# An encoder block on one core: all tiles at the right end of the on-chip memory placed 224 bytes lower

## The chip, the core and the metric

The kernel runs on one core of one Trainium2 chip. The metric is the device time of one execution in microseconds (us), as the median of several runs. The on-chip memory has 128 partitions; an address in this text is a byte offset within a partition, and the same offset holds in all 128. "32 past" means that an address divided by 64 leaves 32, "even" that it leaves 0.

## The reference

One layer on 512 tokens of width 1024, batch 1, all in float32:

```python
xn = rms_norm(h, g_mix);  proj = xn @ w_in                  # (512, 2048)
b_gate, c_gate, v_conv, u_pool = the four 512-wide parts of proj
h = h + concat([b_gate * conv3(c_gate * v_conv), pool_mixer(u_pool)]) @ w_o
xb = rms_norm(h, g_ffn);  q = xb @ w_q                      # 8 heads, 2 halves of 128
s = q . sub_keys                     # 128 keys a half; top 16 of each half, then top 16 of the 256 sums
h = h + sum over the chosen e of softmax(score)_e * gelu(u_e . xb) * v_e     # 16384 experts
h = h + sigmoid(rms_norm(h, g_ple) @ w_ple_gate) * (p @ w_ple_proj)
out = rms_norm(h, g_final)
```

## The kernel before

Everything is one program, `block_kernel`, for one core. Large products are made from float32 numbers split in two parts: a high part H that ScalarE (ACT) writes in the rounded format fp32r, and a low part L = raw - H that VectorE (DVE) writes. A product is then three matmuls (`mm3`: H·H at L123, H·L at L125, L·H at L127), or, in `mm3_pair`, two such products with their matmuls interleaved. In a profile row such as `acc<-xH,wH` the first name after the arrow is the tile that TensorE (PE) streams through, the second is the tile that it holds as weights; each matmul has a weight load of its own (PEld).

The stages, in order of time in the profiled execution:

1. **Start and mixer, 0 to about 160 us.** `norm_rows` and `xT_chunk` make the normalised, transposed input in the tiles xH and xL. Eight pieces of w_in (256 columns each: wraw, split into wH and wL) are weights against the streamed xH, xL, 512 columns a matmul (`projT`). The mixers write mixH and mixL. For the output projection the roles turn round: mixH, mixL are weights and the pieces of w_o are streamed, 256 columns a matmul. Beside it `ple` multiplies pT by wp and stores the result from the tiles pleo.
2. **Queries and keys, to about 279 us.** Eight pieces of w_q, again as weights wH, wL against streamed xH, xL with 512 columns; then 16 matmuls a head against the tile keys, and the top-16 searches on DVE.
3. **First pass over the experts, to about 652 us.** 76 blocks of 128 experts: uraw is loaded, split into uH, uL (weights), and xH, xL are streamed, 384 columns a matmul (`score`). In between run the rest of the top-k on DVE, one-hot matmuls (tiles oh, gg) whose result is collected in stage and stored by ACT's queue, and row gathers by POOL into the six buffers gr for one token block of 128.
4. **Second pass, to about 1397 us.** For the other blocks `score` as before; for all 128 blocks `mix`: wH, wL of the pool wq as weights, the halves of vH, vL streamed, 512 columns a matmul, into the results o.
5. **Tail, to the end.** For each of four token blocks 8 transposes (`tail_T`), giving tH and tL as weights, against the split w_gate, which lies in the former places of xH, xL (first half) and uraw, uH, uL (second half): 512 columns a matmul for seven half blocks, and 256 for two quarters of the last block (`tail_gate`, list QS).

**Where tiles lie.** Pools take memory from the left end (low addresses) or, with `side="right"`, from the right end downwards, each pool on the last one that is open. The right end that the allocator gives is byte 229,344, which is 32 past. Most sizes are multiples of 64, so most right tiles begin 32 past; in the mixer's pool wk the tile zb takes 2080 bytes, which is not such a multiple, and the tiles below it (pT to zb) begin even. The name wH stands for two sets of tiles: the pieces of w_in, w_o and w_q (pool w, right), and those of the second pass (pool wq, left).

The order on each engine is set by the scheduler of the framework for stages 1 to 3 (from a model of times) and is program order from the second pass on (`manual_schedule`). The right side's first pool in the code is

```python
    hpool = sh.enter_context(tc.tile_pool(name="h", bufs=1, side="right"))
```

Of the kernel before, what the change touches and what calls it, by code (L numbers as in the profile page):

```python
# [7 lines left out]
F32 = mybir.dt.float32  # L8
# [8 lines left out]
P = 128  # L17
# [43 lines left out]
def block_kernel(ctx: ExitStack, tc: tile.TileContext, x, pT_in, g_cols, w_in, conv_w, pool_w,  # L61
# [4 lines left out]
    consts = ctx.enter_context(tc.tile_pool(name="consts", bufs=1))  # L66
    dram = ctx.enter_context(tc.tile_pool(name="dram", bufs=1, space=bass.MemoryType.DRAM))
    small = ctx.enter_context(tc.tile_pool(name="small", bufs=2))
    sbx = ExitStack()
    xpool = sbx.enter_context(tc.tile_pool(name="xt", bufs=1))  # L70
    sh = ExitStack()
# [926 lines left out]
```

## Time and profile before

| | us |
|---|---|
| median of 3 runs | 1455.18 (1454.88 to 1456.47) |
| the profiled execution | 1454.46 |
| its span (first to last recorded instruction) | 1452.7 |
| PE busy, matmuls | 1430.8 (98%) |
| DVE busy | 1137.7 (78%) |
| ACT busy | 614.5 (42%) |
| POOL busy | 390.7 (27%) |
| mean granted TensorE clock | 0.994 |

Times in rows count from the start of the span. Matmuls overlap in the records, so a matmul's duration (390 ns for 512 columns, say) is not what it costs: that is read from the distance of the starts of consecutive matmuls. A row of the timeline merges equal neighbours (x2).

### The profile page before, as it was taken

The numbers are of one execution on the slowest core, as the hardware profiler recorded it, in microseconds if no ns is written. First come the engines' busy times: TensorE is split into PE (matmuls) and PEld (weight loads), VectorE is DVE, ScalarE is ACT, GpSimd is POOL, SyncE is SP. The second block draws the span as 40 slices with busy tenths as digits, with TensorE's granted clock in tenths as the row PEclk, the third lists the DMA queues.
The fourth block names the chain that finished last, engine by engine and source line by source line (L and its number), as shares of the span: only waits on it lengthen the run. The fifth ranks groups of instructions, "written<-read, shape, count | busy, mean of one in ns | idle before, by whom it ended". The sixth has DMA issues, their size and how long they took to land.

```text
span 1452.7 us, 20601 instructions
## 1 busy us (share of the span) xinstructions
PE 1430.8 (98%) x7785; PEld 1271.6 (88%) x7785; DVE 1137.7 (78%) x2078; ACT 614.5 (42%) x864; POOL 390.7 (27%) x260
## 2 busy tenths in 40 slices
PE   8999999999998999999999999999999999999997
PEld 5789888999998999998999999999998888788886
DVE  5644579899998987879988778888877777776765
ACT  5321533344564665664333333333333334433354
POOL 0000000002132132125766555454443123342000
PEclk9999999999998999999999999999999999999999
DMA  8223730047688899899998999998997899998721
GB/s 302 87 90 104 242 116 30 30 164 279 227 285 268 274 316 326 262 317 347 380 349 323 375 329 339 347 339 324 346 336 273 317 334 333 335 342 324 249 70 73
DMA packets 152083, 381.38 MB, mean 263 GB/s; under 512 B 10928, under 2 KB 72112, under 8 KB 151728
## 3 DMA queue, kind: packets, MB, share of 16 engines
q1 hardware_dynamic: 72400, 211.75, 41.3%
q0 software_dynamic: 36864, 134.23, 25.3%
q10 hardware_dynamic: 42720, 34.08, 7.2%
q8 instruction: 61, 1.00, 0.3%
q14 instruction: 38, 0.31, 0.1%
HBM read 339.92 MB, written 40.11 MB: 262 GB/s over the span
## 4 chain that ended last, share of the span: by engine, by line
PE 71%; DVE 12%; DMA 7%; issue 6%; ACT 2%; POOL 1%; ACTq 1%; SPq 0%; DVEq 0%; POOLq 0%
PE o L127 11%; PE o L123 11%; PE o L125 11%; PE acc L125 6%; PE acc L123 6%; PE acc L127 6%; PE u L127 5%; PE u L123 5%; PE u L125 5%; DMA uraw<-in_u_blk 3%; DVE uL L586 2%; DMA tH<-in_w_gate 2%; POOL gr L536 1%; PE acc L191 1%; PE tp L516 1%
## 5 line engine op out<-in xcount | busy, mean ns | idle before, releaser
L536 POOL DMA_INDIRECT gr<-in_u_rows,eidx x128 | 201.1, 1571 | 652.5 <-DVE tsm L390 334.6
L536 POOL DMA_INDIRECT gr<-in_v_rows,eidx x128 | 189.4, 1480 | 285.2 <-DVE xrow L560 274.5
L125 PE MATMUL o<-vL,wH 128*128 128x512 f32 x768 | 237.2, 390 | 0.7 <-DVE vL L604 0.7
L123 PE MATMUL o<-vH,wH 128*128 128x512 f32 x768 | 237.7, 390 | 0.3 <-ACT wH L685 0.3
L127 PE MATMUL o<-vH,wL 128*128 128x512 f32 x768 | 237.3, 390 | 0.1
L598 ACT ACTIVATE vH<-vraw 128x1024 fp32r<-128x1024 f32 x128 | 135.4, 1058 | 218.3 <-PE o L127 160.8
L123 PE MATMUL acc<-xH,uH 128*128 128x384 f32 x608 | 206.6, 340 | 3.4 <-ACT uH L580 3.4
L604 DVE TENSOR_TENSOR vL<-vraw,vH 128x1024 fp32r<-128x1024 f32 x128 | 156.2, 1221 | 65.2 <-ACT vH L598 64.9
L125 PE MATMUL acc<-xL,uH 128*128 128x384 f32 x608 | 206.8, 340 | 0.0
L127 PE MATMUL acc<-xH,uL 128*128 128x384 f32 x608 | 204.7, 339 | 0.2 <-DVE uL L586 0.2
L580 ACT ACTIVATE uH<-uraw 128x1024 fp32r<-128x1024 f32 x128 | 135.3, 1058 | 100.6 <-DMA uraw<-in_u_blk 64.0
L586 DVE TENSOR_TENSOR uL<-uraw,uH 128x1024 fp32r<-128x1024 f32 x128 | 155.7, 1217 | 24.8 <-ACT uH L580 24.8
L125 PEld LDWEIGHTS o<-vL,wH 128*128 128x128 f32 x768 | 144.0, 188 | 32.3 <-DVE vL L604 1.5
L127 PEld LDWEIGHTS o<-vH,wL 128*128 128x128 f32 x768 | 143.9, 188 | 31.2 <-DVE wL L690 1.0
L560 DVE SCALAR_TENSOR_TENSOR xrow<-gr,gate,xrow 128x1024 f32<-128x1024 f32 x128 | 164.1, 1282 | 5.1 <-DMA xrow<-h_d 4.6
L123 PEld LDWEIGHTS o<-vH,wH 128*128 128x128 f32 x768 | 143.3, 188 | 27.2 <-ACT wH L685 0.7
L556 DVE SCALAR_TENSOR_TENSOR gr<-gr,xrow 128x1024 f32<-128x1024 f32 x128 | 154.3, 1218 | 4.2 <-DMA gr<-in_u_rows,eidx 4.1
L127 PE MATMUL u<-xH,uL 128*128 128x384 f32 x416 | 139.6, 336 | 0.0
L123 PE MATMUL u<-xH,uH 128*128 128x384 f32 x416 | 139.5, 335 | 0.0
L125 PE MATMUL u<-xL,uH 128*128 128x384 f32 x416 | 139.3, 335 | 0.0
L123 PEld LDWEIGHTS acc<-xH,uH 128*128 128x128 f32 x608 | 115.4, 190 | 4.1 <-ACT uH L580 4.1
L127 PEld LDWEIGHTS acc<-xH,uL 128*128 128x128 f32 x608 | 115.1, 189 | 0.8 <-DVE uL L586 0.8
(214 smaller groups left out, 2336.8 us busy)
## 6 DMA issues: line engine op xcount, KB each, us to landing
uraw<-in_u_blk SPq DMA_DIRECT2D x128, 512.0 KB, 5.2
vraw<-in_v_rows SPq DMA_DIRECT2D x128, 512.0 KB, 6.0
G_d<-stage ACTq DMA_DIRECT2D x12, 1664.0 KB, 12.8
gq<-G_d SPq DMA_DIRECT2D x26, 768.0 KB, 7.0
A_d<-a ACTq DMA_DIRECT2D x17, 768.0 KB, 6.0
aq<-A_d SPq DMA_DIRECT2D x17, 768.0 KB, 9.5
wraw<-in_w_in SPq DMA_DIRECT2D x8, 1024.0 KB, 5.8
wraw<-in_w_q SPq DMA_DIRECT2D x8, 1024.0 KB, 5.8
```

The lines of the kernel that those rows point to most:

```text
L123: nc.tensor.matmul(ps, lh, rh, start=start, stop=False)
L125: nc.tensor.matmul(ps, lh, rl, start=False, stop=False)
L127: nc.tensor.matmul(ps, ll, rh, start=False, stop=stop)
L191: nc.tensor.matmul(ps, pT[:, c, t * P:(t + 1) * P], wp[hf][:, c], start=c == 0, stop=c == 1)
L516: nc.tensor.matmul(ps[:, o:o + P], qb[b][:, t * P:(t + 1) * P], keys[:, 2 * hd + b], start=True, stop=True)
L536: nc.gpsimd.indirect_dma_start(out=g, out_offset=None, in_=table, in_offset=bass.IndirectOffsetOnAxis(ap=eidx[:, k:k + 1], axis=0))
L556: ins = nc.vector.scalar_tensor_tensor(g, g, 1.0, xrow, op0=OP.mult, op1=OP.mult, accum_out=act[:, k:k + 1])
L560: ins = nc.vector.scalar_tensor_tensor(accg, g, gate3[:, k - P:k - P + 1], accg, op0=OP.mult, op1=OP.add)
L580: nc.scalar.activation(ublk[i][1], ublk[i][0], AF.Copy)
L586: nc.vector.tensor_tensor(ublk[i][2], raw, uh.bitcast(F32), op=OP.subtract)
L598: nc.scalar.activation(vblk[n][1], vblk[n][0], AF.Copy)
L604: nc.vector.tensor_tensor(vblk[n][2], raw, vh.bitcast(F32), op=OP.subtract)
```

## The change

A pool is opened on the right side ahead of all others, and one tile of 56 float32 numbers (224 bytes a partition) is taken from it and never used. All later right tiles lie 224 bytes lower. Left tiles stay.

```diff
     small = ctx.enter_context(tc.tile_pool(name="small", bufs=2))
+    right = ctx.enter_context(tc.tile_pool(name="right", bufs=1, side="right"))
+    right.tile([P, 56], F32, name="rpad")
     sbx = ExitStack()
```

The byte addresses in the two built programs (first buffer of each; the others follow at multiples of the tile's size):

| tile | use | before | after | |
|---|---|---|---|---|
| wH, wL (pool w) | weights in w_in, w_q; streamed in w_o | 180192, 196576 | 179968, 196352 | 32 past -> even |
| mixH, mixL | weights in w_o | 114656, 131040 | 114432, 130816 | 32 past -> even |
| xs; keys; h | transposes; keys; residual | 147424; 118752; 212960 | 147200; 118528; 212736 | 32 past -> even |
| oh, gg; stage | one-hot matmuls; their store | 112608, 120800; 128992 | 112384, 120576; 128768 | 32 past -> even |
| gr; gres; a4 | gathers; results | 204768; 167904; 155616 | 204544; 167680; 155392 | 32 past -> even |
| tH, tL; gq | weights in the tail; transposes | 176096, 184288; 192480 | 175872, 184064; 192256 | 32 past -> even |
| pT, wp, pleo, pw, inv, pu, pm | mixer | 63232, 67328, 75520, 83712, 85760, 93952, 100288 | each 224 less | even -> 32 past |
| xH, xL; uraw, uH, uL | left | 16128, 32512; 48896, 57088, 69376 | the same | even |
| vraw, vH, vL; wH, wL (pool wq) | left | 81664, 93952, 106240; 130816, 136960 | the same | even |
| ident | streamed in transposes, left | 13984 | the same | 32 past |

The tiles that are "32 past" before lie at 224 above a multiple of 256, and after at a multiple of 256, as the left tiles named do. The instructions of every engine stand in the same order in both programs, with line numbers two higher in the changed one. One wait moves: the left tiles of the top-k and of uL share places with the mixer's right tiles of an earlier stage, and the 224 bytes shift that overlap. On DVE, where stage 1 gives way to stage 2, before:

```order
L586 TENSOR_TENSOR uL<-uraw,uH 128x1024 [waits DMAHW4_49,Activation_49]
L139 SCALAR_TENSOR_TENSOR xL<-g,gcol,xH 128x512 [waits Activation_49]
L139 SCALAR_TENSOR_TENSOR xL<-tp,gcol,xH 128x512 [waits Activation_49]
L335 TENSOR_TENSOR xrow<-xs 128x1024 [waits DMAHW6_49,DVE_49]
L586 TENSOR_TENSOR uL<-uraw,uH 128x1024 [waits DMAHW3_49,DMAHW5_49,DMAHW2_49,Activation_49]
L586 TENSOR_TENSOR uL<-uraw,uH 128x1024 [waits DMAHW7_49,Activation_49]
L97 TENSOR_TENSOR wL<-wraw,wH 128x2048 [waits DMAHW1_49,PE_49,Activation_49]
L348 MAX tv<-s 128x8 [waits DMAHW0_49,Activation_49]
```

and now the same place:

```order
L588 TENSOR_TENSOR uL<-uraw,uH 128x1024 [waits DMAHW4_49,Activation_49]
L141 SCALAR_TENSOR_TENSOR xL<-g,gcol,xH 128x512 [waits Activation_49]
L141 SCALAR_TENSOR_TENSOR xL<-tp,gcol,xH 128x512 [waits Activation_49]
L337 TENSOR_TENSOR xrow<-xs 128x1024 [waits DMAHW6_49,DVE_49]
L588 TENSOR_TENSOR uL<-uraw,uH 128x1024 [waits DMAHW3_49,DMAHW2_49,DMAHW5_49,DMAHW0_49,Activation_49]
L588 TENSOR_TENSOR uL<-uraw,uH 128x1024 [waits DMAHW7_49,Activation_49]
L99 TENSOR_TENSOR wL<-wraw,wH 128x2048 [waits DMAHW1_49,PE_49,Activation_49]
L350 MAX tv<-s 128x8 [waits Activation_49]
```

The wait for one DMA semaphore (DMAHW0) stands three rows earlier, at the second of the three uL shown instead of the first MAX; it belongs to a store of pleo to memory, whose place the new uL now touches.

## The prediction, made before the changed kernel ran

> **What bounds the kernel now.** I read the page's busy times and chain first, then who waits for whom on PE, then the starts of single matmuls in the timeline, stage by stage.
>
> ```profile
> span 1452.7 us, 20601 instructions
> PE 1430.8 (98%) x7785; PEld 1271.6 (88%) x7785; DVE 1137.7 (78%) x2078; ACT 614.5 (42%) x864; POOL 390.7 (27%) x260
> PE 71%; DVE 12%; DMA 7%; issue 6%; ACT 2%; POOL 1%; ACTq 1%; SPq 0%; DVEq 0%; POOLq 0%
> ...
> PE acc L191 <- DMA wp<-in_w_proj: 7.0, 1, 7.0
> PE acc L123 <- ACT uH L580: 3.4, 3, 2.6
> PE g L470 <- ACT stage L477: 1.4, 4, 0.4
> ```
>
> PE is busy for 1430.8 of 1452.7 us. Of what it waits for, 7.0 us is the first load and 3.4 us three late uH; no other entry is above 1.4. So DVE, ACT and transfers matter only where they make PE wait, and the time is the sum of the matmuls' starting distances. The change adds and moves no instruction, so it can only act through a price that depends on an address. The question is which operation has one.
>
> **Engines and transfers: no sign of a price.** DVE and ACT rows exist with all tiles even, and with tiles 32 past:
>
> ```profile
> L586 DVE TENSOR_TENSOR uL<-uraw,uH 128x1024 fp32r<-128x1024 f32 x128 | 155.7, 1217 | 24.8 <-ACT uH L580 24.8
> L556 DVE SCALAR_TENSOR_TENSOR gr<-gr,xrow 128x1024 f32<-128x1024 f32 x128 | 154.3, 1218 | 4.2 <-DMA gr<-in_u_rows,eidx 4.1
> L580 ACT ACTIVATE uH<-uraw 128x1024 fp32r<-128x1024 f32 x128 | 135.3, 1058 | 100.6 <-DMA uraw<-in_u_blk 64.0
> L113 ACT ACTIVATE xs<-h 128x1024 f32<-128x1024 f32 x8 | 8.4, 1054 | 10.5 <-DMA h<-in_x 6.0 <-DVE h L316 3.2 <-DVE nt L106 1.4
> ```
>
> uL (all even) takes 1217 ns, the pass over gr (read and written 32 past) 1218; uH (even) 1058, xs from h (both 32 past) 1054. So 0 for DVE and ACT, with at most 4 ns an instruction either way, hidden under PE. For transfers, the queues:
>
> ```profile
> q1 hardware_dynamic: 72400, 211.75, 41.3%
> q0 software_dynamic: 36864, 134.23, 25.3%
> q10 hardware_dynamic: 42720, 34.08, 7.2%
> ```
>
> A share is of 16 engines over 1452.7 us. POOL's gathers (q0, all into gr, 32 past) cost 0.253 x 16 x 1452.7 / 134.23 = 43.8 us of engine time per MB; q1, mostly loads into even tiles, 45.3. So 0 for the gathers. ACT's queue (q10, stores from right tiles, mostly in pieces of 512 bytes) costs 49.1, 8% above q1: if all of that were the address, the 3.4 us of waits for uH are the most that it could give back directly. I take 0.
>
> **Matmuls: here the rows differ.** First and last rows of undisturbed stretches, two each: w_in, second pass, tail with 512 columns, tail with 256, w_o, first pass, and the second pass's very end.
>
> ```profile
> 86.07 0.63 PE L123 MATMUL acc<-xH,wH 128*128 128x512 f32 x2
> 97.74 0.63 PE L125 MATMUL acc<-xL,wH 128*128 128x512 f32 x2
> ...
> 1129.99 0.62 PE L123 MATMUL o<-vH,wH 128*128 128x512 f32 x2
> 1141.32 0.62 PE L125 MATMUL o<-vL,wH 128*128 128x512 f32 x2
> ...
> 1423.78 0.40 PE L125 MATMUL o<-xL,tH 128*128 128x512 f32 x1
> 1436.85 0.40 PE L123 MATMUL o<-xH,tH 128*128 128x512 f32 x1
> ...
> 1440.82 0.28 PE L125 MATMUL o<-uL,tH 128*128 128x256 f32 x1
> 1444.43 0.28 PE L127 MATMUL u<-uH,tL 128*128 128x256 f32 x1
> ...
> 139.75 0.28 PE L125 MATMUL acc<-wL,mixH 128*128 128x256 f32 x1
> 140.95 0.28 PE L127 MATMUL acc<-wH,mixL 128*128 128x256 f32 x1
> ...
> 299.75 0.33 PE L125 MATMUL acc<-xL,uH 128*128 128x384 f32 x1
> 301.83 0.33 PE L125 MATMUL acc<-xL,uH 128*128 128x384 f32 x1
> ...
> 1394.89 0.62 PE L125 MATMUL o<-vL,wH 128*128 128x512 f32 x2
> 1396.71 0.62 PE L127 MATMUL o<-vH,wL 128*128 128x512 f32 x2
> ```
>
> - w_in: 25 pairs between the rows, 11.67 us / 50 = 233.4 ns a matmul. Weights 32 past, streamed tile even.
> - Second pass: also 25 pairs, 11.33 / 50 = 226.6. Both even.
> - Tail, 512 columns: 56 steps, 13.07 / 56 = 233.4. Weights 32 past, streamed even.
> - Tail, 256 columns: 31 steps, 3.61 / 31 = 116.5. Weights 32 past, streamed even.
> - w_o, 256 columns: 10 steps, 120.0. Both 32 past.
> - First pass, 384 columns: 12 steps, 2.08 / 12 = 173.3. Both even.
>
> Two lines come out. Where both tiles stand alike, 512, 384 and 256 columns cost 226.6, 173.3 and 120.0: 53.3 for each 128 columns, and w_o, with both 32 past, lies on it. Where only the weights are 32 past, 512 and 256 cost 233.4 and 116.5, a straight rate that is dearer by 6.8 at 512 and cheaper by 3.5 at 256. Surroundings do not explain it: the last mix matmuls run at 4 pairs in 1.82 us, 227.5 each, in the same quiet end where the tail has 233.4. Output banks do not (second pass and tail both write o), nor the streamed tile's name (x in the w_in pieces, u and uraw too in the tail). What the dear stretches share is the weights' address.
>
> **The change, term by term.** Afterwards wH, wL, tH, tL are even, the streamed tiles stay even, so I price them on the first line.
> 1. Weights of w_in and w_q: 768 matmuls of 512 columns (8 + 8 pieces x 2 halves x 8 x 3; the group rows of L123, L125 and L127 have 256 each) x 6.8 ns = -5.2 us.
> 2. Tail, 512 columns: 7 half blocks x 24 = 168, x 6.8 = -1.1 us.
> 3. Tail, 256 columns: 48, x 3.5 = +0.2 us.
> 4. w_o, keys, one-hot: both tiles move together; the first lies on the line already. 0.
> 5. The 64 + 32 transposes (xs, gq even afterwards, ident stays 32 past) come to stand unlike, and the mixer's pT, wp, pw, pm go from even to 32 past together. No row prices either; by the 3% (6.8 of 226.6) between the lines, either way, on some 30 us of PE time (17.3 of it L191): 0, with ±0.9 as bounds.
> 6. The moved DVE wait:
>
> ```profile
> L193 SPq DMA_DIRECT2D ple_d<-pleo x4: 319/320/320, 163.8 to 168.7; - x4
> DMA to landing us min/median/max: 5.8/5.9/7.9
> ...
> 181.00 1.22 DVE L586 TENSOR_TENSOR uL<-uraw,uH 128x1024 fp32r<-128x1024 f32 x1
> ```
>
> The last of these stores is issued at 168.7 and lands at most 7.9 us later, at 176.6; the uL that now waits for it starts at 181.00. I take 0. Were the store late, this uL, the next one, wL and the top-k would stand behind it on DVE, and PE would wait for that wL.
>
> Does the first 5.2 us reach the end? DVE could eat it, since it is nearly full when the first pass starts:
>
> ```profile
> 268.00:281.00 13.00, 13.00 (x74) 11.95 (x73) 10.31 (x71) 3.53 (x6) 0.00 (x0) 1.00 0.00 1
> 281.00:294.00 13.00, 13.00 (x77) 13.00 (x76) 13.00 (x82) 5.79 (x8) 0.00 (x0) 1.00 0.31 93
> 279.10 0.88 DVE L348 MAX8 tv<-s 128x8 f32<-128x128 f32 x4 [2.69 <-ACT s L518]
> ```
>
> (columns: PE, PEld, DVE, ACT, POOL busy). Until 281 DVE has idle time (10.31 of 13.00) and at 279.10 it has waited 2.69 us for the last head's scores, which come from PE through ACT. So DVE's full stretch starts when PE lets it, and slides with PE; the loads of uraw follow the buffers that DVE frees. I take the whole.
>
> Sum: -5.2 - 1.1 + 0.2 = -6.1 us, on the profiled execution's 1454.46: 1448.4. The median of the runs is 0.7 above that execution, so 1455.2 - 6.1 = 1449.1.
>
> **What may disturb it** is one place in the first pass:
>
> ```profile
> 445.00:450.00 5.00, 2.76 (x27) 2.28 (x25) 4.66 (x9) 1.82 (x2) 2.75 (x2) 0.99 0.95 392
> 450.00:455.00 5.00, 4.31 (x23) 3.87 (x24) 3.69 (x5) 4.55 (x10) 0.07 (x1) 0.50 0.97 337
> 455.00:460.00 5.00, 5.00 (x26) 5.00 (x25) 4.59 (x6) 0.51 (x2) 1.28 (x1) 0.82 1.08 322
> 460.00:465.00 5.00, 4.41 (x35) 3.85 (x34) 1.18 (x2) 2.11 (x4) 0.40 (x1) 1.00 0.55 183
> 465.00:470.00 5.00, 4.11 (x25) 3.82 (x25) 5.00 (x8) 3.95 (x8) 0.66 (x1) 0.70 0.56 194
> ```
>
> PE idles 2.24 + 0.69 + 0.59 + 0.89 = 4.4 us here (late uH and uL behind slow loads; DMA share 0.95 to 1.08), and the granted clock falls to 0.50, 0.82 and 0.70 for stretches of 5 us: another 2.5 + 0.9 + 1.5 = 4.9 lost. The place as a whole costs 9.3 us, and hangs on when loads meet stores. A shift by 5 us may soften or double it.
>
> **The rivals.**
> - *No effect.* The weights' address is only what the dear stretches happen to share; their place in the upper half of the memory, or something of the split tiles, makes the 6.8. Then nothing moves: 1455.2. For it: no row shows the same two tiles at two offsets. Against: seven stretches on two lines. [...]
> - *The stores get cheaper too.* If a start at a multiple of 256 shortens the stage stores, uraw lands earlier and the place at 445 to 470 vanishes: 1449.1 - 9.3 = 1439.8. For it: 8% on q10. Against: that 8% goes as well with the small pieces. [...]
> - *Slower.* The first pass starts 5 us earlier, loads and stores meet otherwise in it, and the place at 445 to 470 comes twice: 1449.1 + 9.3 = 1458.4. It decides as soon as what it adds exceeds the 6.1 saved. For it: uL there is late by little; against: everything that feeds it slides together.
>
> **How the numbers follow.** The forecast has 0.62, no effect 0.22, cheaper stores 0.08, slower 0.08. The likeliest case alone runs from 1446 to 1452 (terms 5 and part of the 9.3). The range takes in no effect up to the highest run shown, and leaves out the two last cases: 1444 to 1456.4. A difference under 0.2% (2.9 us) can't be told from none. Faster: 0.62 + 0.08, less 0.02 where the disturbed place eats most of it: 0.68. Slower: 0.08 and a little of no effect: 0.09. The rest, 0.23, is the same.
>
> **What would show it.** Right: starting distances of 226 to 227 ns in w_in, w_q and the tail, 120 in the tail's 256 columns, w_o unchanged, and the first score some 5 us earlier. Wrong in the step "weights' address": 233 stays. Wrong in the step "it reaches the end": 227 appears, but the gain is gone by 660 us, with more idle PE or half clock between 350 and 650. A new distance in w_o, keys or one-hot would show that standing alike is not what counts.

## The result, and the profile after

The changed kernel takes 1447.79 us (median of 7 runs, 1446.25 to 1451.91) against 1455.27 for the kernel before (7 runs beside it): ratio 0.9944, interval 0.993 to 0.9957, which by the ratio is 8.1 us less (6.3 to 10.2); the two medians are 7.5 us apart. The forecast was 1449.1. The profiled execution took 1447.79.

From the page of the changed kernel (span, busy times, queues) and the view of who waits for whom on PE:

```profile
span 1446.0 us, 20600 instructions
PE 1422.0 (98%) x7785; PEld 1267.6 (88%) x7785; DVE 1137.4 (79%) x2078; ACT 612.7 (42%) x864; POOL 381.1 (26%) x260
q1 hardware_dynamic: 72400, 211.75, 41.0%
q0 software_dynamic: 36864, 134.23, 25.4%
q10 hardware_dynamic: 42720, 34.08, 7.0%
...
PE acc L193 <- DMA wp<-in_w_proj: 6.9, 1, 6.9
PE g L472 <- ACT stage L479: 2.9, 8, 0.7
PE acc L125 <- ACT uH L582: 2.9, 4, 1.7
```

PE is 8.8 us less busy. DVE and ACT stand where they were, and the three queues within 0.3 points. The starts of matmuls in the timeline (start, duration), in the places shown of before: w_in, second pass, tail with 512 columns, tail with 256, w_o.

```profile
86.06 0.62 PE L127 MATMUL acc<-xL,wH 128*128 128x512 f32 x2
97.40 0.39 PE L129 MATMUL acc<-xH,wL 128*128 128x512 f32 x1
...
1123.18 0.61 PE L125 MATMUL o<-vH,wH 128*128 128x512 f32 x2
1134.06 0.61 PE L125 MATMUL o<-vH,wH 128*128 128x512 f32 x2
...
1417.12 0.39 PE L125 MATMUL o<-xH,tH 128*128 128x512 f32 x1
1430.71 0.39 PE L125 MATMUL o<-xH,tH 128*128 128x512 f32 x1
...
1433.75 0.28 PE L129 MATMUL o<-uH,tL 128*128 128x256 f32 x1
1437.11 0.28 PE L125 MATMUL u<-uH,tH 128*128 128x256 f32 x1
...
136.88 0.28 PE L129 MATMUL acc<-wH,mixL 128*128 128x256 f32 x1
138.32 0.28 PE L129 MATMUL acc<-wH,mixL 128*128 128x256 f32 x1
```

w_in goes from 233.4 to 11.34 / 50 = 226.8 ns, the tail from 233.4 to 13.59 / 60 = 226.5 and at 256 columns from 116.5 to 3.36 / 28 = 120.0. The second pass stays (10.88 / 48 = 226.7), and w_o too (1.44 / 12 = 120.0). These are the numbers that the prediction gave for tiles that stand alike.

Where the span's 6.7 us come from, by the first matmul of each stage (first w_in, first score, first row of the second pass, first of the tail, last of all). Before:

```profile
18.84 0.47 PE L123 MATMUL acc<-xH,wH 128*128 128x512 f32 x1
273.31 0.33 PE L123 MATMUL acc<-xH,uH 128*128 128x384 f32 x1
660.21 0.63 PE L123 MATMUL o<-vH,wH 128*128 128x512 f32 x2
1397.95 0.48 PE L123 MATMUL o<-xH,tH 128*128 128x512 f32 x1
1444.43 0.28 PE L127 MATMUL u<-uH,tL 128*128 128x256 f32 x1
```

and after:

```profile
18.55 0.48 PE L125 MATMUL acc<-xH,wH 128*128 128x512 f32 x1
268.40 0.33 PE L125 MATMUL acc<-xH,uH 128*128 128x384 f32 x1
653.40 0.63 PE L125 MATMUL o<-vH,wH 128*128 128x512 f32 x2
1392.08 0.48 PE L125 MATMUL o<-xH,tH 128*128 128x512 f32 x1
1437.71 0.28 PE L129 MATMUL u<-uH,tL 128*128 128x256 f32 x1
```

So -0.29 us ahead of w_in, -4.62 in w_in, w_o and w_q (254.47 to 249.85), -1.90 in the first pass, +0.94 in the second, -0.85 in the tail. The experiments ask two things: what rule of addresses lies behind the 6.6 ns, and whether the 1.90 and 0.94 belong to the change.

### The profile page after: what moved, and what is told of

The parts are those of the page before. It is cut to its first block, busy times and chain, and to the rows that moved or that the text cites. A ratio compares the mean times of both kernels' runs of the same rounds, so it can differ in the third digit from the quotient of the medians.

```text
span 1446.0 us, 20600 instructions
## 1 busy us (share of the span) xinstructions
PE 1422.0 (98%) x7785; PEld 1267.6 (88%) x7785; DVE 1137.4 (79%) x2078; ACT 612.7 (42%) x864; POOL 381.1 (26%) x260
## 4 chain that ended last, share of the span: by engine, by line
PE 48%; DVE 4%; DMA 4%; issue 2%; ACT 1%; SPq 0%; DVEq 0%; ACTq 0%
PE o L125 10%; PE o L129 10%; PE o L127 10%; PE u L129 5%; PE u L125 5%; PE u L127 5%; DMA tH<-in_w_gate 4%; DVE vL L606 2%; DVE xrow L562 1%; PE acc L127 1%; PE acc L129 1%; DVE aq L682 1%; PE acc L125 1%; DVE wL L692 0%; ACT xH L98 0%
## 5 line engine op out<-in xcount | busy, mean ns | idle before, releaser
L538 POOL DMA_INDIRECT gr<-in_u_rows,eidx x128 | 197.1, 1540 | 649.7 <-DVE tsm L392 329.7
L538 POOL DMA_INDIRECT gr<-in_v_rows,eidx x128 | 183.9, 1437 | 292.4 <-DVE xrow L562 281.7
L588 DVE TENSOR_TENSOR uL<-uraw,uH 128x1024 fp32r<-128x1024 f32 x128 | 155.8, 1218 | 29.8 <-ACT uH L582 29.4
L558 DVE SCALAR_TENSOR_TENSOR gr<-gr,xrow 128x1024 f32<-128x1024 f32 x128 | 154.3, 1218 | 2.5 <-DMA gr<-in_u_rows,eidx 2.5
```

Of the source, the lines that this page charges most:

```text
L538: nc.gpsimd.indirect_dma_start(out=g, out_offset=None, in_=table, in_offset=bass.IndirectOffsetOnAxis(ap=eidx[:, k:k + 1], axis=0))
L558: ins = nc.vector.scalar_tensor_tensor(g, g, 1.0, xrow, op0=OP.mult, op1=OP.mult, accum_out=act[:, k:k + 1])
L588: nc.vector.tensor_tensor(ublk[i][2], raw, uh.bitcast(F32), op=OP.subtract)
```

## The experiments

The stages of their profiled executions, in us, each number the difference of two starts read as above. The kernels are described one by one below; after_again is the changed kernel once more, and mix32_timed is the kernel of mix32_again once more. Two tiles are called like when their starts leave the same remainder against 64 bytes, and unlike when they don't. A ratio is a kernel's time over that of the kernel before in runs beside it, with its 95% interval in brackets.

| kernel | first w_in to first score | first pass | second pass | tail |
|---|---|---|---|---|
| before | 254.47 | 386.90 | 737.74 | 46.48 |
| after | 249.85 | 385.00 | 738.68 | 45.63 |
| after_again | 249.84 | 386.65 | 738.28 | 45.63 |
| early | 249.97 | 385.49 | 739.26 | 46.48 |
| late | 254.36 | 385.92 | 735.76 | 45.63 |
| left32 | 251.30 | 387.03 | 739.27 | 45.87 |
| w2_unlike | 254.48 | 384.13 | 748.92 | 46.48 |
| mix32 | 249.95 | 383.34 | 737.99 | 45.63 |
| mix32_again | 248.63 | 384.06 | 735.31 | 45.63 |
| mix32_timed | 248.64 | 386.05 | 738.02 | 45.63 |
| mix64 | 248.92 | 387.14 | 738.53 | 45.63 |

**1. Matmuls alone, first grid.**

```
for w, s in pairs: 24 x matmul(bank[r % 2], W[w][:, slice r % 4], S[s], start=True, stop=True)
```

> A kernel of matmuls alone, 24 in a row of each kind, over weights (letter after w) and streamed tiles (letter after s) that start 0, 4, 8, 16, 32, 48, 64 or 128 bytes (a to h) past a multiple of 64; its output leaves out the whole block and is mostly x. Theory 'alike' (what counts is whether both tiles stand the same way against 64 bytes): the pairs aa, dd, ee, ff at 512 columns take 226.6 ns each and every unlike pair 233.4; at 256 columns alike 120.0, unlike 116.5; at 384 alike 173.3 and unlike 175.0 (on the straight rate of 0.456 ns a column); ag, ga, gg, ah, ha as aa. Theory 'weights alone' (only the weights' start counts): all pairs with a in front 226.6, and all with e in front 233.4, ee too. Theory '256 bytes' (a larger grid counts): ag, ga, ah or ha come out at 233.4. Theory 'no address' (the name or the stage made the 6.8 ns): all pairs the same.

Each kind begins where the row of its first matmul starts, so the next kind's start less its own, over 24, is its price (in a row: streamed tile, then weights):

```profile
63.62 0.39 PE L100 MATMUL pu<-sd,wd 128*128 128x512 f32 x1
69.20 0.40 PE L100 MATMUL pu<-se,wd 128*128 128x512 f32 x1
...
85.85 0.39 PE L100 MATMUL pu<-sd,we 128*128 128x512 f32 x1
91.45 0.39 PE L100 MATMUL pu<-se,we 128*128 128x512 f32 x1
96.91 0.39 PE L100 MATMUL pu<-sf,we 128*128 128x512 f32 x1
```

With the same weights 32 past, an unlike stream costs 233.3 (sd) and the like one 227.5 (se): "weights alone" and "no address" fall. But sd,wd, both 16 past, costs 232.5 where "alike" wanted 226.6, and starts 64 bytes apart do not cost the same as 0: 229.0 with the stream ahead, 233.3 with the weights ahead. So against 64 is not the rule. With tiles in the two-byte format f16 the starts 0 and 32 past cost the same within 0.5: 216.3 for the first pair, 215.8 for the other three.

**2. Second grid: the distance in steps of 32 bytes.** Only the starts differ from the first.

> Matmuls alone once more (the output leaves out the whole block), now over the distance of the two starts: letters a to p stand for 0 to 480 bytes in steps of 32 past a multiple of 512, x, y and z for 0 in tiles elsewhere. First the streamed tile is moved, then the weights, then both together; the first series comes again at the end in reverse order. Theory '64 bytes' (alike against 64 is enough): a, c, e, g, ... all at 226.6 ns for 512 columns, the others at 233.4. Theory '256 bytes' (the distance against 256 counts, as 229 ns with a distance of 64 bytes and 232 with 128 in the first grid say): a and i at 227, c and k at 229, e and m at 232, the rest 233; both moved together 227 throughout. Theory '512 bytes': i is unlike too, near 233. Theory 'not the distance' (what ran before, or the place in the bank, decides): the series at the end differs from the first by more than 2 ns in several places, or x, y, z differ from a. At 256 columns the unlike ones come out at 117 instead of 120, at 384 columns at 173 to 176.

The stream moved up by 0 to 288 bytes over fixed weights:

```profile
40.36 0.40 PE L90 MATMUL pu<-sb,wa 128*128 128x512 f32 x1
45.97 0.40 PE L90 MATMUL pu<-sc,wa 128*128 128x512 f32 x1
51.47 0.40 PE L90 MATMUL pu<-sd,wa 128*128 128x512 f32 x1
...
79.50 0.39 PE L90 MATMUL pu<-si,wa 128*128 128x512 f32 x1
84.96 0.40 PE L90 MATMUL pu<-sj,wa 128*128 128x512 f32 x1
...
218.68 0.39 PE L90 MATMUL pu<-sb,wb 128*128 128x512 f32 x1
295.31 0.39 PE L90 MATMUL pu<-sp,wp 128*128 128x512 f32 x1
```

+32 bytes: 5.61 / 24 = 233.8 ns; +64: 229.2; +96 to +224 (sd to sh, five kinds): 28.03 / 120 = 233.6; +256 (si): 227.5, as at 0. From +256 to +480 the numbers of 0 to +224 come again within 0.3 ns. Moved together by 32 to 480 bytes the pair stays at 76.63 / (14 x 24) = 228.1. Moving the weights instead gives the mirror image, and the tiles x, y, z elsewhere 226.7 to 227.8. So at 512 columns and steps of 32 bytes what counts is **the distance of the two starts, against 256 bytes**; the "64 bytes" and "512 bytes" theories fall. The series in reverse order agreed within 1.2 ns, so "not the distance" falls too. At 256 columns unlike starts cost 113 to 120 against 119.5, at 384 columns 173 to 177 against 174. There the rule is less strict: at 256 columns the same distance, made by moving the stream or the weights, came out up to 3 ns apart (117.3 with the stream 160 ahead, 120.2 with the weights 96 ahead, which is the same against 256). The first grid also has 448 columns, where two equal starts cost 203.1 (both 0 past) and 206.7 (both 32 past).

**3. The other way round.**

```
+    consts.tile([P, 8], F32, name="lpad")     # first tile on the left
```

> The other way round: nothing moves on the right, and all tiles on the left move up by 32 bytes, so that both sides start 32 past a multiple of 64; only the transposes stand unlike (ident even, xs and gq 32 past). Alike: 227 ns in w_in, w_q and the tail, 120 in the tail's 256 columns, 226.6 in the second pass, 173.3 in the first: some 1449 us, like the full change. Weights alone: 233.4 in the second pass too, 2304 x 6.8 = 15.7 us more, and nothing gained: 1471 us or more. No address: 1455.3. If even starts as such make transfers cheaper, the 1.5 us beyond 6.1 are missing here.

Ratio 0.997 (0.9951 to 0.9989). Both sides now start 32 past 64, but the streamed x stands 64 bytes ahead of w against 256. In w_in:

```profile
86.00 0.62 PE L124 MATMUL acc<-xH,wH 128*128 128x512 f32 x2
96.98 0.62 PE L124 MATMUL acc<-xH,wH 128*128 128x512 f32 x2
```

10.98 / 48 = 228.8, near the grid's 229.2 for +64, and the stage gains 3.2 us in place of 4.6. My "alike" theory missed here; "weights alone" missed by more, since the second pass did not rise.

**4. Half of the change at a time.**

```
early:  pad of 224 bytes opened ahead of wpool (closed with stage two)
late:   pad of 224 bytes opened ahead of gat (after stage two)
```

> Only the tiles of stages one and two move down by 224 bytes; everything that is opened later on the right (gathered rows, stage, gq, tH, tL) and h stays 32 past. Alike and weights alone: 227 ns in w_in and w_q, 233 and 116.5 in the tail, -5.2 us, some 1450.0 us. If what the full change gave beyond 6.1 us comes from the stores and gathers of the first pass standing on even starts, nothing of it is here: 1450.0. If it comes from the first pass starting 5 us earlier (so that the stretch of half clock at 450 us does not come), it is all here: 1448.5. No address: 1455.3.

> Only what is opened on the right after the second stage moves down by 224 bytes (gathered rows, stage, gres, a4, gq, tH, tL); weights of w_in and w_q stay 32 past. Alike and weights alone: 233 in w_in and w_q, 227 and 120 in the tail, -0.95 us, some 1454.3 us, not to be told from no change. If the stores and gathers of the first pass are cheaper on even starts: that and 1.5 us more, 1452.8, and no half clock near 450 us. If the earlier start of the first pass made the rest: 1454.3 with the half clock still there.

Early: 0.9951 (0.9932 to 0.9971); late: 0.9985 (0.9967 to 1.0003). The table gives what the times can't: early has the whole gain up to the first score and an unchanged tail, late the opposite, and neither has a first pass unlike the others. The stores of the first pass moved in late and not in early, and the two first passes are 0.4 us apart, so nothing of cheaper stores shows there. That the granted clock fell near 450 us in late too (0.73 between 450 and 460; 0.93 over 430 to 480, 3.5 us lost) says little by itself, since that comes and goes (see 8).

**5. The second pass made unlike**, to test the price where it is large enough to show in the time.

```
+    lp.tile([P, 8], F32, name="lpad")     # between v tiles and wH, wL of the second pass
```

> The kernel before with 32 bytes put between the second pass's v tiles and its weights wH and wL, so that these 2304 matmuls, alike before, stand 32 bytes apart; nothing else is touched. If the distance of the two tiles sets the price and PE bounds this pass: 233.3 ns in place of 226.6, 2304 x 6.7 = 15.4 us more, some 1469.5 us. If the price belongs to the first stages or to tiles from the right end: no change, 1454. If pass two has slack that hides a dearer matmul: 233.3 ns, but less than 8 us at the end.

1465.88 us, ratio 1.0079 (1.0048 to 1.011): 11.5 us more, 7 to 16. The trace in the middle of the pass:

```profile
1130.97 0.63 PE L123 MATMUL o<-vH,wH 128*128 128x512 f32 x2
1142.17 0.63 PE L123 MATMUL o<-vH,wH 128*128 128x512 f32 x2
```

11.20 / 48 = 233.3. The second pass grew by 11.2 us where 15.4 was expected. The starts of the rows show where the missing 4 us are. The pass has 50 short runs of 18 mix matmuls between scores, and two long runs. One short run of before, by its first and ninth matmul and the first of the score behind it:

```profile
746.92 0.63 PE L123 MATMUL o<-vH,wH 128*128 128x512 f32 x2
748.77 0.62 PE L125 MATMUL o<-vL,wH 128*128 128x512 f32 x2
751.04 0.33 PE L123 MATMUL u<-xH,uH 128*128 128x384 f32 x1
```

The first eight cost 1.85 / 8 = 231 ns each, the ten behind them 2.27 / 10 = 227. Over all 52 runs the first nine average 231.4 ns in before and 233.1 in w2_unlike, the next eight 226.7 and 233.3: a like pair takes its low price only after some nine matmuls in a row. So 52 x 9 = 468 matmuls grew by 1.7 ns instead of 6.6, and 2.3 us are missing there. Most of the rest are waits in the long run of 1260 mix matmuls: its steps of over 250 ns exceed 227 by 2.2 us in before and by 0.7 in w2_unlike. They are 3.2 us in after, which is the +0.94 above, 0.4 in late and none in mix32_again, so this part of the spread of the second pass is waiting and not a price.

**6. w_o.** mix32 was to move mixH and mixL by 32 bytes:

```
mix32:        mpool pad of 32 bytes ahead of mixH
mix32_again:  mpool pad of 32 bytes behind mixL      mix64:  of 192 bytes
```

> The changed kernel with mixH and mixL (and what lies below them: mixer tiles, keys) another 32 bytes lower, so that w_o, alike in both kernels at 120.0 ns for 256 columns, stands unlike. Distance theory: 117 ns, 384 x 3 = 1.2 us less than the full change, which the time can hardly tell (some 1447 us), the starts of the matmuls can. If only the weights' own start counts, or nothing does: 120.0 stays.

It did not: the pool puts its first tile lowest, so the pad came to lie below, mixH stayed, and w_o stayed at 120.0. Only the mixer's tiles below it moved (the keys did not, since their pool is opened after the mixer's are closed), and nothing followed (1449.28 us, 0.9966, 0.9948 to 0.9984).

> The changed kernel with 32 bytes put above mixH and mixL inside their pool, so that this time the two tiles do move (in mix32 the bytes came to lie below them, and they stayed where they were). w_o's streamed weights stand +32 from them. By the grid 118 ns, by the tail of the kernel before 116.5, for 120.0: 384 x 2.0 to 3.5 = 0.8 to 1.3 us less in w_o. If accumulating in one bank undoes it, 120.0.

> The changed kernel with 192 bytes above mixH and mixL, so that w_o's streamed tiles stand 64 bytes before them, the cheapest distance of the grid at 256 columns (113.4 and 115.1 ns in its two forms). Distance theory: 384 x 4.9 to 6.6 = 1.9 to 2.5 us less than the full change in w_o, some 1445.5 us, the first w_q matmul that much earlier. If the grid's order of slices made its value: 120.0, 1447.8.

> The kernel of mix32_again, timed. Its trace has w_o 1.26 us shorter than the full change (44.69 for 45.95 us from the first matmul to the last) and its single time, 1442.17, lay far below anything that explains. If only w_o counts: the full change's 0.9956 and 1.3 us less, a ratio of 0.9947, some 1447 us. If the 32 bytes also calm the first pass: 1444 or less, a ratio below 0.993.

First and last matmul of w_o in mix32_again:

```profile
111.46 0.28 PE L125 MATMUL acc<-wH,mixH 128*128 128x256 f32 x1
156.15 0.28 PE L129 MATMUL acc<-wH,mixL 128*128 128x256 f32 x1
```

44.69 / 383 = 116.7 ns, as the tail had before; after has 45.95. That is 1.26 us, as expected. mix64 gives 45.11 (117.8), not the grid's 113.5: its cheapest distance did not carry over, and why stays open. Timed, mix32_timed took 1446.99 (0.994, 0.9921 to 0.996) and mix64 1447.67 (0.9947, 0.9928 to 0.9967). By its stages the former is the best kernel here, but no time shown can tell it from the full change; the 1442.17 of mix32_again did not come again in six runs of the same kernel (1445.59 to 1451.02), and its trace is the one without waits in the second pass's long run.

**7. Narrower weights.**

```
matmul(bank[r % 2][:m, :n], W[w][:, c*P:c*P + m], S[s][:, :n])      # m = 128, 96, 64, 32
```

> Matmuls alone (the output leaves out the whole block) with weights of 128, 96, 64 and 32 columns, at 512 and 256 streamed columns and the distances 0, +32, -32, +64 and -64 bytes. Theory 'weight load meets stream' (the load of the next weights and the stream of the current matmul get in each other's way, and the distance decides how): what unlike pairs pay over like ones at 512 columns, 6.7 ns with 128 columns of weights, shrinks with them to some 3.4 at 64 and 1.7 at 32. Theory 'the stream alone': 6.7 ns at every width.

With 128 columns the grid repeats (like 227, 32 bytes apart 233). With 96:

```profile
77.42 0.39 PE L90 MATMUL pu<-sa,wa 128*96 128x512 f32 x1
82.94 0.39 PE L90 MATMUL pu<-sb,wa 128*96 128x512 f32 x1
88.38 0.39 PE L90 MATMUL pu<-sa,wb 128*96 128x512 f32 x1
```

Here the like pair costs 230.0 and the pair with the stream 32 bytes ahead 226.7: the order is reversed. At 64 and 32 columns all lie between 228 and 236, like ones at 230 and 231. Both theories fail in their numbers. Which distance is cheap changes with the number of weight columns, so the stream alone does not set it. That number is also the number of output rows, and no run tells the load of the weights from the output; how they meet stays open.

**8. The full change again.**

> The full change again, beside mix64 on one chip and with more runs. The working gives -6.1 us; the first comparison -7.5. If the rest was the chance of few runs of the kernel before, this lies nearer to 6; if the change does something that the working lacks, it stays at 7.5.

1448.4 us, 0.9956 (0.9942 to 0.997): 6.4 us less, 4.4 to 8.4. Its stages repeat those of after within 0.01 us up to the first score and in the tail; the first pass took 1.65 us more, so most of the -1.90 of the first comparison did not come again, and nothing shows that it belongs to the change.

That leaves the first pass. The stretch of the disturbed place (PE, PEld, DVE, ACT, POOL busy, granted clock, DMA share, GB/s) in before, after, w2_unlike and mix64:

```profile
430.00:480.00 50.00, 45.40 (x304) 42.80 (x303) 43.76 (x59) 28.00 (x50) 14.26 (x9) 0.90 0.82 273
```

```profile
430.00:480.00 50.00, 45.79 (x344) 43.20 (x343) 45.52 (x59) 27.62 (x49) 11.95 (x9) 1.00 0.86 279
```

```profile
430.00:480.00 50.00, 46.09 (x342) 43.47 (x342) 46.30 (x62) 29.87 (x53) 13.53 (x9) 1.00 0.91 295
```

```profile
430.00:480.00 50.00, 44.94 (x301) 42.51 (x301) 42.32 (x57) 24.88 (x45) 10.75 (x8) 0.90 0.84 268
```

PE idles 3.9 to 5.1 us in all four. The lowered clock costs (1 - 0.90) x 50 = 5.0 us in before and none in w2_unlike, whose tiles up to here stand exactly as in before; none in after and 5.0 in mix64, whose tiles stand as in after here (only mixH, mixL and what lay below them had moved, all closed by then). The changed kernel itself lost none in after and 1.5 us in after_again. So it comes and goes by execution. In all eleven traces the losses are 0, 1.5, 3.5 or 5.0 us. In before the clock stands at 0.50 for 6.83 us (449.94 to 456.77) and again for 3.4 us (467.0 to 470.4). An estimate from these two stretches: half of the shorter, half of the longer and half of both are 1.7, 3.4 and 5.1 us, and the losses agree with that within the 0.25 us that the clock's two decimals leave. What brings the clock down is not shown: PE idles much alike in all four stretches above, and in two of them the clock stays at 1.00.

## Why the prediction was right, point by point

- **"The question is which operation has a price that depends on an address": matmuls only.** Held for what reaches the end. DVE and ACT did not move (the pass over gr takes 1218 ns in both kernels, xs from h 1054). The stores did, a little: ACT's queue takes 7.0% of the span in all seven kernels whose stores start at a multiple of 256, and 7.1 to 7.3% in the four where they start 224 above one, some 3% less. The prediction's 0 for them stands in the time: the first pass averages 385.5 us in the seven and 385.9 in the four.
- **Terms 1 to 3.** The prices came out at 6.6 ns for 6.8 in quiet stretches, and +3.5 in the tail's 256 columns. Term 1 gave -4.6 us for -5.2: over the whole stage a matmul gained 4.62 / 768 = 6.0. By the starts in the two traces, 590 of the 768 gained 6.6 ns, and the 178 that stand within nine of a break (a wait, or another kind of matmul between) only 4.3, as in the short runs of w2_unlike. The prediction took the quiet price for all of them. Terms 2 and 3 gave -0.85 for -0.95.
- **Term 4.** 0, as said; mix32_again shows that w_o's "0" was a choice of distance and not a law.
- **Term 5.** The first w_in starts 0.29 us earlier, inside ±0.9; kernels that leave those tiles alone (late, w2_unlike) have 18.70 and 18.77 against 18.84 in before, and early, which moves the same tiles of the first stage (xs and the mixer's), has 18.73. So no run shows that the 0.29 belongs to these tiles.
- **Term 6.** 0: the uL that now waits for the store follows its predecessor directly.

```profile
176.97 1.22 DVE L337 TENSOR_TENSOR xrow<-xs 128x1024 f32<-128x1024 f32 x1
178.12 1.22 DVE L588 TENSOR_TENSOR uL<-uraw,uH 128x1024 fp32r<-128x1024 f32 x1
```

- **"I take the whole": it reaches the end.** Held. The first score comes 4.9 us earlier, and DVE still waits for the last head's scores from PE through ACT (2.52 us, for 2.69 before):

```profile
274.19 0.88 DVE L350 MAX8 tv<-s 128x8 f32<-128x128 f32 x4 [2.52 <-ACT s L520]
```

- **The rule.** "Both tiles stand alike", which the prediction read against 64 bytes, was too loose a reading of seven stretches: it holds against 256. The forecast survived because 224 bytes make the distance 0 against both; for a pad of 32 bytes it would have failed, as left32 shows.
- **The sum.** -6.1, against -5.5 by the two stages that repeat and -8.1 (6.3 to 10.2) and -6.4 (4.4 to 8.4) in two comparisons: the forecast gain lies just under the first interval and inside the second. What goes beyond 5.5 is not accounted for by any stage: the first pass ran 383.3 to 387.1 us over all profiled kernels, in no order with the change.
- **The rivals.** No effect: refuted by rows at two offsets. Cheaper stores: they are cheaper by some 3%, and the disturbed place stayed (PE idles 4.2 us between 430 and 480 for 4.6 before). Slower: the place did not come twice.

## What to carry to other kernels

When like instructions run at two prices, lay out which operands they share before naming the property, and then sweep that property alone: seven stretches fitted "alike against 64", and one sweep of 24 matmuls per step gave 256. Where PE bounds a kernel of fp32r matmuls with 512 streamed and 128 weight columns in long runs, try letting weights and stream start at the same place against 256 bytes: it was worth 2.9% of each such matmul here (226.7 for 233.3 ns), and little in the first nine of a run. A gain below the spread of the runs (15 us from the lowest to the highest of 26 runs of before) is read from starts in the trace that repeat, not from the time.

## What the runs showed of the hardware that I had not expected

- At 512 columns the price depends on the distance with a period of 256 bytes and not evenly: 227.5 at 0, 229.2 with the stream 64 ahead, 233 to 234 elsewhere. At 256 columns equal starts are among the dear cases (119.5, with others from 113.5 to 120.2).
- The low price of equal starts sets in only after some nine matmuls: 231.4 ns before that and 226.7 after, over 52 runs of the second pass.
- Starts at 4, 16 and 48 bytes do not follow the distance: both 4 past cost 237.6, both 16 past 232.5, and weights 48 past with a stream 16 past 227.0.
- f16 showed no dependence at 512 columns (215.8 ns) or 128 (55.8), plain f32 none either (429 ns a record at 512 columns, two records a matmul), fp32r with 128 columns none (111.7).
